# A decoder layer on one core: the scaling of the softmax weights of kv head 0, from DVE to ACT

## The chip, the core and the metric

The kernel runs on one core of one Trainium2 chip. Its engines work side by side, each through its own queue: PE (TensorE, matrix products), DVE (VectorE, element by element), ACT (ScalarE, functions and copies with a scale), POOL (GpSimd) and SP (SyncE, which here issues the DMA transfers). They meet at semaphores. The metric is the device time of one execution in microseconds (us).

## What is computed

One layer: sliding-window attention and a short gated convolution side by side, merged by gates, then a gated feed-forward part. The change lies in the attention, with 8 query heads over 2 kv heads (4 query heads, `g`, to each kv head), blocks of 128 queries against 256 keys (the block before and its own), a band mask, and one more logit per head (the sink) in the softmax. Cut to that part:

```python
SEQ = 2048; HEAD_DIM = 64; N_HEADS = 8; N_KV_HEADS = 2; GROUP = 4; WINDOW = BLOCK = 128

scores = jnp.einsum("bnqhgd,bnkhd->bnhgqk", q, kw).astype(jnp.float32) * ATTN_SCALE
scores = jnp.where(mask[None, :, None, None], scores, -jnp.inf)
probs = jax.nn.softmax(jnp.concatenate([scores, sink], axis=-1), axis=-1)[..., :-1]
out = jnp.einsum("bnhgqk,bnkhd->bnqhgd", probs.astype(v.dtype), vw)
```

## The kernel before

Everything is float32; products are made from a high and a low part of each operand, in three matmuls (`mm3`, L247 to L249; `split` makes the two parts, a cast on ACT at L264 and a subtraction on DVE at L265). The sequence is cut into four chunks of 512 tokens. The kernel runs in stages: projections of the input (to about 700 us of the trace), four mixers, one to a chunk (to about 1130 us), the feed-forward part (the rest, PE nearly full all the way).

A mixer (`mixer`) goes over the chunk's four blocks of 128 queries. For block `b` it writes down `scores` of block `b`, then `weights_to_keys` and `attend` of block `b - 1`, and between these a number of steps of other work by a hand-written plan: the output projection of the chunk before (`out_proj`, tiles `wo`) and the conv branch of this chunk (`conv_steps`, tiles `brc`). Chunk 0 has no chunk before it, so its plan has the eight conv steps alone. When all four blocks are done, `attn_steps` multiplies the result with the attention branch's weights (tiles `bra`), gates it and splits it into `merged`. The weights of all these steps come by DMA, are split on ACT and DVE (tiles `wh`), and are fetched up to three tiles ahead.

`scores` takes the products of queries and keys in PSUM (`sc`), scales and masks them into `s` on DVE (L565; one tile `s` of 128 queries x 4 heads x 257 for each kv head, with the sink in the last column). For each kv head then: the maximum of each row, negated, on DVE (L574); `exp(s + m)` on ACT, a head at a time, with the sum of each row as a by-product (L576); the reciprocal of the sums on DVE (L578); and the scaling of the weights by it. For kv head 0 this is one multiply over all four heads on DVE (L580), for kv head 1 four copies with a scale on ACT (L584). In the first block of chunk 0 there are no earlier keys, so 128 columns to a head are scaled instead of 256. `weights_to_keys` turns the weights over on PE (L594) and splits them (`pts`), ACT and DVE again. `attend` multiplies them with the values (`po`, L607), adds the two halves of the result with a copy on ACT (L609) and an addition on DVE (L610) into `o`, and splits `o` into `attn`.

The program's text gives the dependencies; the order in which each engine takes its instructions is laid out by a planner when the kernel is built, with its own estimate of each instruction's time. An engine takes its instructions in that order and waits where the next one isn't ready. The tiles `s` and `pts` share a pool of eight buffers (`b4`); PSUM has eight.

Of the kernel before, what the change touches and what calls it, by code (L numbers as in the profile page):

```python
# [23 lines left out]
ALU = mybir.AluOpType  # L24
AF = mybir.ActivationFunctionType
AX = mybir.AxisListType

P = 128
# [6 lines left out]
NH, HD, G = 8, 64, 4  # L35
# [61 lines left out]
def layer_kernel(ctx: ExitStack, tc: tile.TileContext, x, w, bcol, g1, g2, gf, cw, fcw, sinks, out):  # L97
    nc = tc.nc
# [10 lines left out]
    def psum(name):  # L109
        return p_ps.tile([P, 512], F32, name=name, tag="ps")  # L110
# [440 lines left out]
    def scores(c, q, b):  # L551

        k0 = P if c == 0 and b == 0 else 0
        keys = slice(b * P + k0, b * P + 256)
        qs = slice(b * P, (b + 1) * P)
        ss = [pool["b4"].tile([P, G, 257], F32, name=f"s{c}_{b}_{kv}", tag="b4") for kv in range(2)]
        for kv in range(2):
            nc.scalar.copy(out=ss[kv][:, :, 256], in_=sinkb[:, kv * G:(kv + 1) * G])
        for hp in range(2):
            for kv in range(2):  # L560
                ps = psum(f"sc{c}_{b}_{hp}_{kv}").rearrange("p (h n) -> p h n", h=2)
                for h in range(2):
                    nc.tensor.matmul(ps[:, h, k0:], q[:, kv, hp * 2 + h, qs], kT[:, kv, keys], start=True, stop=False)
                    nc.tensor.matmul(ps[:, h, k0:], q[:, kv, hp * 2 + h, qs], kT[:, 2 + kv, keys], start=False, stop=True)
                nc.vector.scalar_tensor_tensor(out=ss[kv][:, hp * 2:hp * 2 + 2, k0:256], in0=ps[:, :, k0:],  # L565
                                               scalar=SCALE, in1=mask[:, None, k0:].to_broadcast([P, 2, 256 - k0]),
                                               op0=ALU.mult, op1=ALU.add)
        for kv in range(2):
            s = ss[kv]
            nm = f"{c}_{b}_{kv}"  # L570
            m = p_s.tile([P, G], F32, name=f"m{nm}", tag="m")
            den = p_s.tile([P, G], F32, name=f"den{nm}", tag="den")
            rden = p_s.tile([P, G], F32, name=f"rden{nm}", tag="rden")
            nc.vector.tensor_reduce(out=m, in_=s[:, :, k0:], axis=AX.X, op=ALU.max, negate=True)  # L574
            for g in range(G):
                nc.scalar.activation(out=s[:, g, k0:], in_=s[:, g, k0:], func=AF.Exp, bias=m[:, g:g + 1],  # L576
                                     accum_out=den[:, g:g + 1])
            nc.vector.reciprocal(out=rden, in_=den)  # L578
            if kv == 0:
                nc.vector.tensor_tensor(out=s[:, :, k0:256], in0=s[:, :, k0:256],  # L580
                                        in1=rden[:, :, None].to_broadcast([P, G, 256 - k0]), op=ALU.mult)
            else:
                for g in range(G):
                    nc.scalar.activation(out=s[:, g, k0:256], in_=s[:, g, k0:256], func=AF.Copy, scale=rden[:, g:g + 1])  # L584
        return ss

    def weights_to_keys(c, b, ss):
# [55 lines left out]
    def mixer(c, q, vT, conv, merged, beside):  # L643
# [12 lines left out]
        steps(plan[0])  # L656
        turn_v(c, vT)
        ss = scores(c, q, 0)
        steps(plan[1])
        for b in range(1, NT):  # L660
            nxt = scores(c, q, b)
            pts = weights_to_keys(c, b - 1, ss)
            steps(plan[2 * b])
            attend(c, b - 1, pts, attn)
            steps(plan[2 * b + 1])
            ss = nxt
# [404 lines left out]
```

## Time and profile before

| | us |
|---|---|
| median of 3 runs | 2549.35 |
| lowest of the runs | 2546.07 |
| the profiled execution | 2549.61 |
| its span, first to last instruction | 2546.4 |

One run of the three took 4931.02 us; the median does not rest on it.

In the profile's rows, a time in front is the start of an instruction (or of a group of like ones, `x4`) from the start of the span, and the next number how long the group took. In groups by line, the numbers behind the bar are the busy time of the group and the mean of one instruction in ns, then the idle time of the engine just before its instructions and what ended it. `out<-in` names the tiles. PEld is PE's loading of weights, which runs beside its matmuls. Instructions of one engine overlap a little: the next may begin before the last one ends.

### The profile page before, as it was taken

What the parts mean: (1) busy time and instruction counts of PE and PEld (TensorE: products, weight loads), DVE (VectorE), ACT (ScalarE), POOL (GpSimd) and SP (SyncE); (2) the same over time, 40 slices, a digit from 0 to 9 for tenths busy, and PEclk for the clock granted to TensorE, in tenths of its full rate; (3) what the DMA queues carried; (4) which work ended last, traced back from release to release, by engine and by line L of the source; (5) the groups of instructions that cost most, each with busy time, mean ns of one, the idle gap of its engine ahead of it and who ended that gap; (6) DMA issues with size and microseconds to landing.
All of it is one profiled execution on the core that took longest, in us unless ns stands there. A gap on an engine that the chain in (4) does not pass through costs nothing.

```text
span 2546.4 us, 30318 instructions
## 1 busy us (share of the span) xinstructions
PE 2470.5 (97%) x11032; PEld 2029.7 (80%) x11032; DVE 1782.3 (70%) x2282; ACT 1118.2 (44%) x1843; POOL 22.6 (1%) x72
## 2 busy tenths in 40 slices
PE   7999999999989998998999999999999999999998
PEld 6888787888868787876788888888888888888886
DVE  6977746664388676677788888755478888875335
ACT  5545544444466353544555555422135555551001
POOL 0000000000000000000000000000000000000000
PEclk9999999999999999999999999999999999999999
DMA  4656897233568868688543233788463332356421
GB/s 154 192 184 206 272 345 226 92 108 100 176 223 306 285 236 288 229 272 306 207 151 131 100 117 115 294 319 295 175 231 124 109 123 100 108 191 258 179 83 66
DMA packets 191221, 488.66 MB, mean 192 GB/s; under 512 B 22112, under 2 KB 41696, under 8 KB 181728
## 3 DMA queue, kind: packets, MB, share of 16 engines
q1 hardware_dynamic: 191072, 486.73, 55.1%
q8 instruction: 86, 1.41, 0.2%
q14 instruction: 63, 0.52, 0.1%
HBM read 325.17 MB, written 161.48 MB: 191 GB/s over the span
## 4 chain that ended last, share of the span: by engine, by line
PE 81%; DMA 7%; DVE 5%; ACT 3%; issue 3%; SPq 2%; POOL 0%; POOLq 0%; DVEq 0%; ACTq 0%
PE upx L792 10%; PE upx L793 9%; PE upx L794 9%; PE dn L249 6%; PE dn L247 6%; PE dn L248 6%; PE upz L794 5%; PE upz L792 5%; PE upz L793 5%; PE upy L793 2%; PE upy L792 2%; PE upy L794 2%; DMA hb<-hd 2%; PE wo L247 2%; PE wo L249 2%
## 5 line engine op out<-in xcount | busy, mean ns | idle before, releaser
L792 PE MATMUL upx<-upx,wh 128*128 128x512 f32 x704 | 277.0, 394 | 5.8 <-ACT u L815 3.9
L793 PE MATMUL upx<-upx,wh 128*128 128x512 f32 x704 | 276.2, 392 | 0.0
L794 PE MATMUL upx<-upx,wh 128*128 128x512 f32 x704 | 275.9, 392 | 0.1
L247 PE MATMUL dn<-act,wh 128*128 128x512 f32 x704 | 274.3, 390 | 0.0
L249 PE MATMUL dn<-act,wh 128*128 128x512 f32 x704 | 274.0, 389 | 0.0
L248 PE MATMUL dn<-act,wh 128*128 128x512 f32 x704 | 273.9, 389 | 0.0
L895 DVE TENSOR_TENSOR hr<-dn,hr 128x512 f32<-128x512 f32 x192 | 131.3, 689 | 199.3 <-PE dn L249 199.1
L853 DVE SCALAR_TENSOR_TENSOR a<-u,fcwc,a 128x1024 f32<-128x1024 f32 x176 | 224.0, 1282 | 49.8 <-ACT a L851 47.0
L264 ACT CAST wh<-ws 128x1024 fp32r<-128x1024 f32 (+1 forms) x150 | 124.9, 834 | 142.3 <-DVE ws L207 67.1
L264 ACT CAST wh<-wr 128x1024 fp32r<-128x1024 f32 (+1 forms) x72 | 69.6, 975 | 261.4 <-PE dn L249 218.9
L792 PE MATMUL upx<-x,wh 128*128 128x512 f32 x440 | 173.2, 394 | 6.5 <-ACT u L824 3.6
L265 DVE TENSOR_TENSOR wh<-ws,wh 128x1024 fp32r<-128x1024 f32 (+1 forms) x150 | 143.1, 955 | 45.5 <-ACT wh L264 45.2
L793 PE MATMUL upx<-x,wh 128*128 128x512 f32 x440 | 172.2, 391 | 0.0
L794 PE MATMUL upx<-x,wh 128*128 128x512 f32 x440 | 172.1, 391 | 0.1
L792 PEld LDWEIGHTS upx<-upx,wh 128*128 128x128 f32 x704 | 132.6, 188 | 37.2 <-ACT u L815 4.3
L794 PEld LDWEIGHTS upx<-upx,wh 128*128 128x128 f32 x704 | 132.5, 188 | 29.8 <-DVE wh L265 0.5
L793 PEld LDWEIGHTS upx<-upx,wh 128*128 128x128 f32 x704 | 132.5, 188 | 28.4
L248 PEld LDWEIGHTS dn<-act,wh 128*128 128x128 f32 x704 | 132.2, 188 | 27.6
L249 PEld LDWEIGHTS dn<-act,wh 128*128 128x128 f32 x704 | 132.1, 188 | 27.6
L247 PEld LDWEIGHTS dn<-act,wh 128*128 128x128 f32 x704 | 132.1, 188 | 27.0
L793 PE MATMUL upz<-upx,wh 128*128 128x512 f32 x352 | 137.1, 389 | 0.8 <-DVE upx L265 0.8
L792 PE MATMUL upz<-upx,wh 128*128 128x512 f32 x352 | 137.1, 389 | 0.0
(274 smaller groups left out, 5394.4 us busy)
## 6 DMA issues: line engine op xcount, KB each, us to landing
act<-actd SPq DMA_DIRECT2D x20, 2048.0 KB, 9.5
wrb<-in_w_dram SPq DMA_DIRECT2D x75, 512.0 KB, 3.7
wra<-in_w_dram SPq DMA_DIRECT2D x75, 512.0 KB, 3.7
wr<-in_w_dram SPq DMA_DIRECT2D x64, 512.0 KB, 5.9
actd<-ach SPq DMA_DIRECT2D x88, 256.0 KB, 2.2
actd<-acl SPq DMA_DIRECT2D x88, 256.0 KB, 2.4
upx<-upd SPq DMA_DIRECT2D x10, 2048.0 KB, 9.7
sgd<-u SPq DMA_DIRECT2D x64, 256.0 KB, 2.9
```

The costliest lines, as they stand in the source:

```text
L247: nc.tensor.matmul(ps, ah, bh, start=start, stop=False)
L248: nc.tensor.matmul(ps, ah, bl, start=False, stop=False)
L249: nc.tensor.matmul(ps, al, bh, start=False, stop=stop)
L264: nc.scalar.copy(out=dh, in_=src)
L265: nc.vector.tensor_sub(out=dl, in0=src, in1=dh.bitcast(F32))
L792: nc.tensor.matmul(bank, ah, bh, start=start and k == 0, stop=False, skip_group_check=True)
L793: nc.tensor.matmul(bank, ah, bl, start=False, stop=False, skip_group_check=True)
L794: nc.tensor.matmul(bank, al, bh, start=False, stop=stop and k == 3, skip_group_check=True)
L853: nc.vector.scalar_tensor_tensor(out=a, in0=u[:, k:k + 2 * T], scalar=w3[k], in1=a, op0=ALU.mult, op1=ALU.add)
L895: nc.vector.tensor_tensor(out=hs[n][j], in0=ps, in1=hs[n][j], op=ALU.add)
```

## The change

The distinction between the two kv heads is gone: both are scaled by four copies on ACT, each with the head's reciprocal as its scale.

```diff
             nc.vector.reciprocal(out=rden, in_=den)
-            if kv == 0:
-                nc.vector.tensor_tensor(out=s[:, :, k0:256], in0=s[:, :, k0:256],
-                                        in1=rden[:, :, None].to_broadcast([P, G, 256 - k0]), op=ALU.mult)
-            else:
-                for g in range(G):
-                    nc.scalar.activation(out=s[:, g, k0:256], in_=s[:, g, k0:256], func=AF.Copy, scale=rden[:, g:g + 1])
+            for g in range(G):
+                nc.scalar.activation(out=s[:, g, k0:256], in_=s[:, g, k0:256], func=AF.Copy, scale=rden[:, g:g + 1])
         return ss
```

There are 16 blocks (four chunks of four), so 16 multiplies on DVE go and 64 copies on ACT come.

## The prediction

> **What bounds the kernel now.** I read the page first, then busy time by windows over the part in which the changed lines run, then the lists of ACT, DVE and PE in order of time. Of the page:
>
> ```profile
> span 2546.4 us, 30318 instructions
> PE 2470.5 (97%) x11032; PEld 2029.7 (80%) x11032; DVE 1782.3 (70%) x2282; ACT 1118.2 (44%) x1843; POOL 22.6 (1%) x72
> PE 81%; DMA 7%; DVE 5%; ACT 3%; issue 3%; SPq 2%; POOL 0%; POOLq 0%; DVEq 0%; ACTq 0%
> ```
>
> TensorE is busy 97% of the span and carries 81% of the chain that ended last. DVE is busier than ACT (70% against 44%), but DVE has only 5% of the chain and ACT 3%, so moving work between them is worth what happens in those few places. The changed lines run between 708 and 1110 us, in the four mixers. Windows over the attention part of each (chunk 0, 1, 2, 3), then over three stretches between chunks (columns: window, its length, busy us and instructions of PE, PE's weight loads, DVE, ACT and POOL, granted clock, busy share of the DMA engines, GB/s):
>
> ```profile
> 708.00:757.00 49.00, 37.83 (x192) 28.83 (x192) 44.08 (x71) 40.07 (x121) 0.00 (x0) 0.97 0.57 203
> 777.00:865.00 88.00, 87.86 (x450) 73.75 (x450) 72.28 (x108) 56.97 (x145) 1.38 (x1) 1.00 0.82 287
> 900.00:988.00 88.00, 88.00 (x457) 74.66 (x457) 63.66 (x99) 50.97 (x137) 1.39 (x1) 1.00 0.68 237
> 1020.00:1110.00 90.00, 89.33 (x463) 76.00 (x464) 66.02 (x103) 50.09 (x132) 1.38 (x1) 1.00 0.65 229
> ```
> ```profile
> 865.00:890.00 25.00, 19.75 (x77) 14.79 (x76) 14.25 (x22) 3.00 (x5) 0.00 (x0) 0.93 0.89 304
> 965.00:1015.00 50.00, 43.45 (x192) 34.69 (x193) 31.44 (x51) 15.07 (x37) 1.39 (x1) 0.97 0.91 319
> 1115.00:1165.00 50.00, 43.83 (x176) 34.78 (x175) 37.77 (x54) 20.23 (x30) 0.00 (x0) 0.93 0.88 300
> ```
>
> Two kinds of attention stage. In chunks 1 to 3 PE has no room to gain: 0.14, 0.00 and 0.67 us idle, because the plan puts the last chunk's output projection and the conv branch beside the softmax. In chunk 0 that filling is thin: PE stands 11.2 of 49 us, DVE is busy 44.1 and ACT 40.1. There the softmax itself sets the time. Between chunks PE waits with the DMA engines busy 88 to 91%; the change touches no transfer.
>
> **The instructions and their prices.** Groups by line, shapes kept apart:
>
> ```profile
> L584 ACT ACTIVATE s<-s,rden 128x256 f32<-128x256 f32 x60 | 25.6, 498 | 0.5 <-DVE rden L578 0.5
> L580 DVE TENSOR_TENSOR s<-s,rden 128x1024 f32<-128x1024 f32 x15 | 18.2, 1216 | 0.1
> ```
> ```profile
> L580 DVE TENSOR_TENSOR s<-s,rden x16: 679/1214/1225, 712.7 to 1088.4; 128x1024 f32<-128x1024 f32 x15, 128x512 f32<-128x512 f32 x1
> ```
> ```profile
> 713.52 1.28 ACT L584 ACTIVATE s<-s,rden 128x128 f32<-128x128 f32 x4 [0.39 <-DVE rden L578]
> ```
>
> Removed: 16 DVE multiplies (L580), 15 of 1.22 us and one, half as wide, of 0.68 (block 0 of chunk 0, which has no earlier keys). Added: 64 ACT copies with a scale, 60 of 128x256 and four of 128x128. One takes 498 ns by itself but they overlap: 25.6 us for 60 is 0.43 each, and four in the list below go from 722.25 to the next start at 723.86, 1.61 us. So a block costs ACT 1.61 (1.28 for the four narrow ones) and saves DVE 1.22. Over all: DVE 15 x 1.22 + 0.68 = 19.0 us less, ACT 15 x 1.61 + 1.28 = 25.4 us more. No transfer is added, and the function is one that ACT already runs between the exponentials.
>
> [...] Counting that loss against DVE (1.61 - 1.22) as time in each of 16 blocks would give 6.2 us more, 2555.8; that lies within the range that the rows give below.
>
> **Chunk 0, block by block.** ACT's list, blocks 1 and 2 (their exponentials start at 716.95 and 727.79):
>
> ```profile
> 716.47 0.58 ACT L264 CAST pts<-pt 128x512 fp32r<-128x512 f32 x1 [1.21 <-PE pt L594]
> 716.95 0.51 ACT L576 ACTIVATE s<-s,m 128x257 f32<-128x257 f32 x1
> ...
> 721.03 1.19 ACT L609 COPY o<-po 64x512 f32<-64x512 f32 x2
> 722.25 1.71 ACT L584 ACTIVATE s<-s,rden 128x256 f32<-128x256 f32 x4
> 723.86 0.60 ACT L264 CAST attn<-o 128x512 fp32r<-128x512 f32 x1
> ...
> 726.47 0.64 ACT L264 CAST wh<-wr2attn 128x512 fp32r<-128x512 f32 x1
> ...
> 727.79 0.51 ACT L576 ACTIVATE s<-s,m 128x257 f32<-128x257 f32 x1
> ...
> 732.35 1.71 ACT L584 ACTIVATE s<-s,rden 128x256 f32<-128x256 f32 x4
> 734.08 0.58 ACT L609 COPY o<-po 64x512 f32<-64x512 f32 x1
> ...
> 739.85 0.51 ACT L576 ACTIVATE s<-s,m 128x257 f32<-128x257 f32 x1 [2.60 <-DVE m L574]
> ```
>
> and DVE's over block 2:
>
> ```profile
> 730.57 1.22 DVE L580 TENSOR_TENSOR s<-s,rden 128x1024 f32<-128x1024 f32 x1
> 731.87 0.18 DVE L578 RECIPROCAL rden<-den 128x4 f32<-128x4 f32 x1
> ...
> 734.69 0.69 DVE L610 TENSOR_TENSOR o<-po,o 64x512 f32<-64x512 f32 x1 [0.28 <-ACT o L609]
> 735.41 1.29 DVE L565 SCALAR_TENSOR_TENSOR s<-sc,mask 128x512 f32<-128x512 f32 x2
> ...
> 738.61 2.34 DVE L574 TENSOR_REDUCE m<-s 128x4 f32<-128x1028 f32 x2
> ```
>
> The lists are not in the order of the text: both maxima (L574) stand together, and kv 1's exponentials follow kv 0's without waiting. A planner orders each engine. So I do not assume that ACT stops after kv 0's exponentials; the new copies go in after some of kv 1's, when the reciprocal is there. The new wait is ACT's for the reciprocal on DVE; behind it on ACT stand kv 1's exponentials, the o copies and the pts casts, and PE's transposes (L594) wait for those.
>
> Block 0: 1.28 us of copies; ACT then idles 1.21 us before 716.47, waiting for PE, and the 0.39 us wait for the reciprocal, which stands behind the multiply, goes. I take 0, ends 0 and 1.28.
> Block 1: ACT has no idle from 716.95 to 727.79, so 1.61 is the upper end. But the weight casts at 726.47 and behind can slip into the later 2.60 us idle, which leaves about 0.3. I take 0.8.
> Block 2: the loop from one block's exponentials to the next is read backwards: 739.85 waits for the maximum at 738.61, DVE is full back to 734.69, which waited for ACT's o copy at 734.08, which stood behind the copies at 732.35. DVE's multiply at 730.57 is beside this, not on it; the added copies are on it: 1.61. With the multiply gone the last po of the earlier block is ready some 1.2 earlier, and its copy could go ahead of the scale copies: then 0. I take 0.8.
> Block 3 has no later scores; its ACT list has no room:
>
> ```profile
> 743.92 0.58 ACT L609 COPY o<-po 64x512 f32<-64x512 f32 x1
> 744.41 1.71 ACT L584 ACTIVATE s<-s,rden 128x256 f32<-128x256 f32 x4
> ...
> 746.74 1.56 ACT L264 CAST pts<-pt 128x512 fp32r<-128x512 f32 x3
> ```
>
> From the copies the way leads over transposes and casts to the attn cast for which PE waits before the attention branch. I take 1.6, ends 0 and 1.61.
> Gain: if DVE were the only limit of the stage, four multiplies gone are worth 0.68 + 3 x 1.22 = 4.3 us. I take 0, since the backward reading finds none of them on the way; 4.3 is the lower end.
>
> **Chunks 1 to 3.** The first block of chunk 1 is tight:
>
> ```profile
> 791.37 1.71 ACT L584 ACTIVATE s<-s,rden 128x256 f32<-128x256 f32 x4
> ```
> ```profile
> 791.31 2.58 PE L594 MATMUL pt<-ident,s 128*128 128x128 f32 x16
> 793.65 0.48 PE L247 MATMUL wo<-mg,wh 128*128 128x512 f32 x1
> ```
>
> PE's transposes run while the copies are still being made; 1.61 us more on ACT can hold PE 1.61 us, or nothing if the planner puts wo matmuls first. I take 0.8. In the later blocks the cover is large, as chunk 2 shows (copies first, transposes of the same block second):
>
> ```profile
> 912.68 1.69 ACT L584 ACTIVATE s<-s,rden 128x256 f32<-128x256 f32 x4
> ...
> 923.57 1.71 ACT L584 ACTIVATE s<-s,rden 128x256 f32<-128x256 f32 x4 [0.25 <-DVE rden L578]
> ```
> ```profile
> 916.14 1.91 PE L594 MATMUL pt<-ident,s 128*128 128x128 f32 x16
> ```
> ```profile
> 938.22 1.75 PE pt L594 x16
> ```
>
> (The last row is from the chain.) Block 0 has 916.14 - (912.68 + 1.69) = 1.77 us, just more than 1.61, and kv 1's transposes are the later eight; block 1 has 938.2 - 925.3 = 12.9 us. These cost 0. Were that cover gone, each block would cost up to 1.61.
>
> **Sum.** The profiled execution took 2549.6 us, 3.2 around its span of 2546.4; the median of the runs is 2549.35, so it stands for them. 0 + 0.8 + 0.8 + 1.6 + 0.8 = 4.0: 2549.6 + 4.0 = 2553.6. Ends of the direct costs: 2549.6 - 4.3 = 2545.3, and 2549.6 + 1.28 + 4 x 1.61 = 2557.3.
>
> **Rivals.**
> 1. DVE's relief decides chunk 0. For it: DVE is busy 44.1 of 49 us there. Against it: the way back from 739.85 goes through ACT. 2545.3. Chance 0.13.
> 2. Nothing changes: the planner lays the copies into ACT's idle time (1.21 and 2.60 in chunk 0) and moves the o copies ahead. 2549.6. Chance 0.17.
> 3. The planner lays out the rest differently. For it: order is its own, and transfers start when buffers come free. The three stretches between chunks hold 5.3, 6.6 and 6.2 us of PE idle with DMA at 88 to 91%; a changed start of transfers can take away or add some of these 18 us. If half: 2549.6 + 4.0 plus or minus 9, 2544.6 or 2562.6. Chance 0.17, split evenly.
> 4. Slower by far: ACT stands in every block until the reciprocal has come through DVE's queue, behind one maximum (half of 2.34) and two mask additions (1.29), with PE waiting for it. 1.61 + 1.17 + 1.29 + 0.18 = 4.25 in each of 16 blocks, 68 us: 2618. It passes 2% from 3.2 us a block. Against it: the 12.9 us of cover. Chance 0.03.
>
> **How the numbers follow.** The forecast keeps 0.5. Two per cent of 2549 is 51 us, about what a measurement of this kernel can tell from no change; PE's whole idle time is 2546.4 - 2470.5 = 75.9 us, only 11 of it in chunk 0, so a gain of that size has 0.01 at most. Rival 4 gives slower 0.03; all else is within: 0.96. The range of 8 in 10 takes in the direct ends and most of rival 3: 2544 to 2562; the forecast's own is 2549.6 to 2557.3.
>
> **What would show it.** After the change: DVE 18 to 19 us less busy, ACT some 25 us more; 128 scale copies in place of 64; the window of chunk 0's attention 3 us longer with ACT busier than DVE in it; PE idle in chunks 2 and 3 as before. Wrong would be: chunk 0 shorter (rival 1), or chunk 0 unchanged and the difference lying between the chunks or behind 1165 us (rival 3), or transposes in chunks 2 and 3 waiting for scale copies (rival 4).

## The result, and the profile after

| | before | after |
|---|---|---|
| median, us | 2547.93 (5 runs) | 2561.39 (5 runs, 2558.26 to 2566.92) |
| profiled execution, us | 2549.61 | 2562.91 |
| its span, us | 2546.4 | 2560.3 |

The ratio is 1.0052, with a 95% interval of 1.0040 to 1.0063: by 2% the same, but measurably slower, by 13.4 us between the medians. One of the five runs before took 4931.02 us, and two runs of the experiments took over 3500 us (one of them a profile, not used below): the ratios and their intervals leave such runs out.

The page of the changed kernel, span, busy time of the engines and the chain:

```profile
span 2560.3 us, 30359 instructions
PE 2475.7 (97%) x11032; PEld 2033.5 (79%) x11032; DVE 1765.9 (69%) x2266; ACT 1141.6 (45%) x1907; POOL 21.5 (1%) x72
PE 83%; DMA 6%; DVE 4%; ACT 3%; issue 2%; SPq 2%; POOL 0%; POOLq 0%; DVEq 0%; ACTq 0%
```

The change did what it says: DVE has 16.4 us and 16 instructions less, ACT 23.4 us and 64 instructions more. PE's own work is the same, but its busy time is 5.2 us more, a first sign that some of its matmuls ran slower.

Where the time went is read from stages. The attention of a chunk is taken here from the first matmul that turns the values over (`vp`, L548) to the first one of the attention branch (`bra`). Windows over it for chunks 0 and 1, before and then after (start and end of the window, its length, busy us of PE, weight loads, DVE, ACT, POOL, granted clock, share of the DMA engines, GB/s):

```profile
702.83:754.24 51.41, 40.24 (x214) 31.26 (x212) 46.55 (x76) 42.09 (x124) 0.00 (x0) 0.97 0.59 211
776.15:868.33 92.18, 90.86 (x466) 76.08 (x464) 73.79 (x110) 58.02 (x145) 1.38 (x1) 1.00 0.82 292
```
```profile
705.88:759.77 53.89, 40.09 (x214) 31.21 (x212) 42.85 (x72) 48.00 (x140) 0.00 (x0) 0.97 0.57 202
781.70:879.24 97.54, 92.58 (x465) 77.20 (x464) 71.17 (x108) 63.79 (x162) 1.01 (x1) 0.98 0.78 274
```

and for chunks 2 and 3 after:

```profile
912.90:1003.80 90.90, 90.17 (x466) 76.19 (x464) 61.13 (x97) 57.22 (x153) 1.01 (x1) 1.00 0.69 240
1035.60:1125.30 89.70, 89.70 (x466) 76.32 (x464) 61.23 (x98) 55.93 (x147) 1.01 (x1) 1.00 0.64 217
```

Chunk 0 is 2.5 us longer, and ACT is now the busier engine in it (48.0 against 42.9). Chunk 1 is 5.4 us longer: PE idles 4.96 us instead of 1.32, and is busy 1.72 longer with the same matmuls. Chunks 2 and 3 have the lengths that they had (90.8 and 89.7), with 6 us more on ACT each.

Chunk 1 shows how it goes. ACT in order of time: the two groups of copies of block 0 (795.33 for kv head 0, 799.34 for kv head 1), then block 1, of whose exponentials only the first of kv head 1 is shown (those of kv head 0 start at 802.94):

```profile
795.33 1.69 ACT L580 ACTIVATE s<-s,rden 128x256 f32<-128x256 f32 x4
...
799.34 1.71 ACT L580 ACTIVATE s<-s,rden 128x256 f32<-128x256 f32 x4
...
804.92 1.04 ACT L264 CAST pts<-pt 128x512 fp32r<-128x512 f32 x2
805.86 1.71 ACT L580 ACTIVATE s<-s,rden 128x256 f32<-128x256 f32 x4
807.47 0.49 ACT L576 ACTIVATE s<-s,m 128x257 f32<-128x257 f32 x1
...
809.44 0.56 ACT L264 CAST pts<-pt 128x512 fp32r<-128x512 f32 x1
809.91 1.71 ACT L580 ACTIVATE s<-s,rden 128x256 f32<-128x256 f32 x4
```

and PE over the same stretch (what ended an idle time stands in brackets):

```profile
797.35 1.03 PE L590 MATMUL pt<-ident,s 128*128 128x128 f32 x8
799.90 0.44 PE L590 MATMUL pt<-ident,s 128*128 128x128 f32 x2 [1.51 <-ACT s L580]
...
806.34 1.10 PE L603 MATMUL po<-pts,vt 128*128 128x512 f32 x4
810.06 0.62 PE L603 MATMUL po<-pts,vt 128*128 128x512 f32 x1 [2.61 <-ACT pts L264]
810.47 0.63 PE L247 MATMUL wo<-mg,wh 128*128 128x512 f32 x1
810.90 0.63 PE L248 MATMUL wo<-mg,wh 128*128 128x512 f32 x1
```

Two waits. PE has turned over kv head 0 of block 0 and stands 1.51 us for kv head 1's copies, which are late by kv head 0's. Then the third cast of `pts` (block 0, kv head 1), whose transposes were done at about 801, is taken by ACT only at 809.44: the planner has put block 1's scale copies and the exponentials of its kv head 1 ahead of it, 805.86 to 809.44, 3.6 us. PE stands 2.61 us for it. In the kernel before, all four casts stood together ahead of block 1's first exponential:

```profile
794.96 2.00 ACT L264 CAST pts<-pt 128x512 fp32r<-128x512 f32 x4
...
797.76 0.51 ACT L576 ACTIVATE s<-s,m 128x257 f32<-128x257 f32 x1 [0.60 <-DVE m L574]
```

A third part comes behind the second wait. Three windows of 3.4 us, laid where the trace's records of the granted clock change, the first with the wait in it:

```profile
806.90:810.30 3.40, 0.79 (x4) 0.38 (x3) 0.94 (x3) 3.40 (x12) 0.00 (x0) 1.00 0.97 261
810.30:813.70 3.40, 3.40 (x9) 2.65 (x9) 1.76 (x3) 3.38 (x8) 0.00 (x0) 0.50 0.78 307
813.70:817.10 3.40, 3.40 (x16) 2.75 (x16) 2.73 (x5) 2.38 (x6) 0.00 (x0) 1.00 0.62 255
```

After a stretch with PE busy 0.79 of 3.40 us the granted clock is 0.50 for the next 3.4 us; the two `wo` matmuls above start 0.43 us apart, where in the profile before they start 0.23 apart. Nine matmuls pass instead of sixteen: about 1.7 us, as PE's busy time in the stage says too (1.72 more). So 1.51 + 2.61 + 1.7 = 5.8; PE's other idle time in the stage is 0.5 us less than before (0.84 against 1.32), and the stage is 5.4 longer.

### The profile page after: what moved, and what is told of

Its sections match the earlier page's. It is cut to its first block, busy times and chain, and to the rows that moved or that the text cites. A ratio compares the mean times of both kernels' runs of the same rounds, so it can differ in the third digit from the quotient of the medians.

```text
span 2560.3 us, 30359 instructions
## 1 busy us (share of the span) xinstructions
PE 2475.7 (97%) x11032; PEld 2033.5 (79%) x11032; DVE 1765.9 (69%) x2266; ACT 1141.6 (45%) x1907; POOL 21.5 (1%) x72
## 4 chain that ended last, share of the span: by engine, by line
PE 83%; DMA 6%; DVE 4%; ACT 3%; issue 2%; SPq 2%; POOL 0%; POOLq 0%; DVEq 0%; ACTq 0%
PE upx L788 10%; PE upx L789 10%; PE upx L790 10%; PE dn L247 6%; PE dn L248 6%; PE dn L249 6%; PE upz L790 5%; PE upz L788 5%; PE upz L789 5%; PE upy L790 2%; PE upy L789 2%; PE upy L788 2%; PE wo L247 2%; PE wo L249 2%; PE wo L248 2%
```

## The experiments

Theory A: ACT's added copies cost time where PE has nothing else to do until they are through, in chunk 0 and in the first two blocks of chunk 1, and nowhere else. Rival B: the planner's other layout of transfers behind the attention, which any edit brings. Rival C: DVE's relief is worth something. Lengths in us of the stages, as defined above, from each kernel's profile, and the ratios (95% interval) to runs of the kernel before taken beside it:

| kernel | start of chunk 0 | chunk 0 | 1 | 2 | 3 | ratio |
|---|---|---|---|---|---|---|
| before | 702.8 | 51.4 | 92.2 | 90.8 | 89.7 | |
| before_again | 706.4 | 49.9 | 92.3 | 90.7 | 89.6 | a profile alone |
| after | 705.9 | 53.9 | 97.5 | 90.9 | 89.7 | 1.0052 (1.0040 to 1.0063) |
| rep | 705.1 | 56.2 | 97.8 | 91.5 | 89.7 | 1.0049 (1.0030 to 1.0069) |
| c0_only | 706.5 | 56.5 | 92.5 | 91.0 | 89.7 | 1.0023 (1.0011 to 1.0035) |
| c1_only | 705.2 | 50.7 | 97.5 | 91.4 | 89.8 | 1.0019 (1.0006 to 1.0033) |
| c23_only | 708.1 | 51.2 | 92.5 | 91.2 | 89.8 | 1.0010 (0.9998 to 1.0022) |
| pts_first | 709.7 | 56.2 | 93.6 | 91.2 | 89.7 | 1.0023 (1.0013 to 1.0034) |
| c1b0_only | 700.9 | 51.1 | 94.7 | 91.0 | 89.7 | 1.0004 (0.9995 to 1.0014) |
| c1b1_only, profile of c1b1_again | 703.7 | 50.7 | 91.0 | 90.7 | 89.6 | 0.9996 (0.9987 to 1.0005) |
| dve_heads0 | 704.0 | 52.6 | 92.1 | 91.7 | 89.7 | 1.0014 (1.0001 to 1.0027) |
| c0_kv0_unscaled | 705.9 | 50.8 | 91.6 | 90.6 | 89.7 | 1.0003 (0.9994 to 1.0012) |
| c0_kv1_unscaled | 707.0 | 49.5 | 91.3 | 91.1 | 89.6 | 1.0001 (0.9992 to 1.0011) |

**rep**: the changed kernel with four blank lines, so that lines keep their numbers; L584 is then L580.

> The changed kernel once more, with four blank lines so that its line numbers are those of the kernel before. Against the kernel before the changed one took 13.4 us more by the medians. Between the two profiles 2 to 3 us of difference lie ahead of 703 us, where the instructions of all engines stand in the same order. If that part is run-to-run variation, this profile has it at another size (0 to 1 us) and the rest the same: 2.5 us more in the attention of chunk 0, 5.3 in that of chunk 1, about 1.0 in the attention branch of chunk 1, 1.6 between 1113 and 1250 us. If it belongs to the kernel, the 2 to 3 us come again. Time 2558 to 2564 either way.

The 5.4 us of chunk 1 came again (5.6). Chunk 0 was 4.8 longer than in the first profile of before, not 2.5. The start of chunk 0 was later again, by 2.3 us (3.1 the first time), against the 0 to 1 that was expected of variation; before_again, further down, tells what that is. The 1.0 us in the attention branch of chunk 1 did not come again: from its first matmul to the start of chunk 2 it took 32.6 us before, 33.6 after and 30.9 in rep.

**The change in one part of the chunks alone**, three kernels that differ in a condition:

```diff
-            if kv == 0:
+            if kv == 0 and c > 0:      # c0_only
+            if kv == 0 and c != 1:     # c1_only
+            if kv == 0 and c < 2:      # c23_only
```

> Kv head 0 goes to ACT in chunk 0 alone. Theory A (the cost lies where ACT stands in PE's way, in chunk 0 and the first two blocks of chunk 1): 2.5 us more than before, all of it in the attention of chunk 0, so about 2550.5. Rival B (the cost is a different layout of the transfers behind, and any edit brings it): 8 us or more, beyond chunk 0. Rival C (DVE's relief is worth something): less than before.

> Kv head 0 goes to ACT in chunk 1 alone. Theory A: 5.3 us more than before in the attention of chunk 1 (1.5 of PE waiting for a scale copy, 2.6 waiting for a cast of pts behind copies and exponentials on ACT, and slower matmuls right after that wait), and perhaps 1 us in its attention branch: about 2553 to 2554. Rival B: 8 us or more, most of it elsewhere. Rival C: 0 or less.

> Kv head 0 goes to ACT in chunks 2 and 3 alone. Theory A: 0 in the attention of both chunks, since PE has matmuls of the output projection and the conv branch until the copies are done; 2548, within 1.6 for what comes behind. Rival B: 3 us or more, between the chunks or behind 1130 us. A fourth, that every block costs something: 6 us or more in the windows of attention.

Each pays in its own chunk and nowhere else in attention: 56.5 in chunk 0 (twice the 2.5 that was expected), 97.5 in chunk 1, nothing in 2 and 3. The ratios 0.23, 0.19 and 0.10% add up to 13.3 us of 2552, the whole change to 12.5 by rep. So the cost lies in separate places, and rival B is not needed for chunks 0 and 1. The 0.10% of c23_only has zero in its interval; it isn't in the attention of any chunk, and where it lies stays open.

**pts_first**: the changed kernel, with block 0's transposes and casts written down ahead of block 1's softmax, in chunk 1 alone.

```diff
-    def scores(c, q, b):
+    def scores(c, q, b, between=None):
...
+        pts = weights_to_keys(c, b - 1, between) if between else None
         for kv in range(2):
             s = ss[kv]
...
-            nxt = scores(c, q, b)
-            pts = weights_to_keys(c, b - 1, ss)
+            if (c, b) == (1, 1):
+                nxt, pts = scores(c, q, b, ss)
+            else:
+                nxt = scores(c, q, b)
+                pts = weights_to_keys(c, b - 1, ss)
```

> The changed kernel, with one thing moved in chunk 1: the transposes and splits of block 0 (weights_to_keys) are written down before the softmax of block 1, so that ACT takes the four casts of pts before the exponentials and copies of block 1. All 64 copies stay on ACT. Theory A (of the 5.3 us in chunk 1, PE's wait for the third cast of pts, which stands behind four copies and four exponentials on ACT, makes some 4 with the slow matmuls after it): the attention of chunk 1 costs 1.5 us more than before instead of 5.3, and the time is about 4 us under that of the changed kernel. Rival (the copies' time on ACT as such holds PE, wherever they stand): still 4 to 5.3 us. A wait of 2.6 us on a cast of pts must be gone from PE's waits under A.

ACT's list of this kernel in chunk 1, with all four casts together and the exponentials and copies of block 1 behind them:

```profile
809.20 2.01 ACT L264 CAST pts<-pt 128x512 fp32r<-128x512 f32 x4
811.10 0.53 ACT L577 ACTIVATE s<-s,m 128x257 f32<-128x257 f32 x1
...
813.44 1.71 ACT L581 ACTIVATE s<-s,rden 128x256 f32<-128x256 f32 x4
```

and its PE, waits of 0.2 us and more between 782 and 835 us (who waited for what: us in all, times, longest):

```profile
PE pt L594 <- ACT s L581: 1.5, 1, 1.5
PE wo L248 <- DVE mg L265: 0.2, 1, 0.2
```

The 2.6 us wait is gone with the same 64 copies on ACT, and chunk 1 has 93.6 us, 1.5 over the profile of before and 4 under the changed kernel. The place of the copies in ACT's queue made that part, not their time. By the ratios the time is 6.6 us under rep's (0.26%), more than the 4 of the stage; the intervals of the two just overlap (1.0034 and 1.0030). What is left against the kernel before, 0.23% or 5.9 us, is about what chunk 0 and the first wait of chunk 1 cost.

**One block of chunk 1 alone:**

```diff
-            if kv == 0:
+            if kv == 0 and (c, b) != (1, 0):     # c1b0_only
+            if kv == 0 and (c, b) != (1, 1):     # c1b1_only, c1b1_again
```

> Kv head 0 on ACT in block 0 of chunk 1 alone, 4 copies instead of 64. Theory A: block 0's later copies make its transposes late, PE waits 1.5 us for them, and the casts of pts come after block 1's exponentials on ACT (without block 1's copies of kv head 0 in between, 1.6 us less than in the changed kernel). So the attention of chunk 1 is 2.5 to 4 us longer than before; the other stages as before. Rival (each block pays its own copies, 1.6): 1.6 us.

> Kv head 0 on ACT in block 1 of chunk 1 alone. Theory A: block 0's transposes come in time, ACT casts pts before block 1's exponentials, and block 1's copies have 13 us until their transposes: 0 us (within 0.5) in the attention of chunk 1. Rival (each block pays its own copies): 1.6 us.

> Kv head 0 on ACT in block 1 of chunk 1 alone, for an undisturbed profile. Theory A: 0 us (within 0.5) in the attention of chunk 1; rival: 1.6.

Four copies in block 0 cost 2.5 us of chunk 1's length, four in block 1 nothing: there the casts are all ahead of block 1's exponentials, as before, and the stage is even 1.2 us shorter, since PE's wait of 1.2 us for a weight tile at its end is missing in that profile. By their ratios, neither kernel's time differs from the kernel before. ACT's list in c1b0_only, with block 1's first exponential of kv head 1 between the casts, and its PE's waits from 770 to 830 us:

```profile
797.41 1.04 ACT L264 CAST pts<-pt 128x512 fp32r<-128x512 f32 x2
798.35 0.51 ACT L576 ACTIVATE s<-s,m 128x257 f32<-128x257 f32 x1
...
800.34 0.57 ACT L264 CAST pts<-pt 128x512 fp32r<-128x512 f32 x1
```
```profile
PE pt L594 <- ACT s L584: 1.5, 1, 1.5
PE po L607 <- DVE pts L265: 0.8, 1, 0.8
PE wo L248 <- DVE mg L265: 0.4, 1, 0.4
```

Here too the casts were put behind block 1's exponentials, but without block 1's extra copies the wait is 0.8 instead of 2.6. So block 0's lateness brings both the first wait and the bad order, and block 1's copies make the second wait long: alone the two blocks cost 2.5 and 0, together 5.4. The rival, that each block pays 1.6 us for its own copies, fails on block 1, which alone costs nothing.

**Chunk 0 from the other sides.** Both heads on DVE there, a head at a time (kv head 0 of the other chunks too):

```diff
-            if kv == 0:
-                nc.vector.tensor_tensor(...)
-            else:
-                for g in range(G):
+            for g in range(G):
+                if kv == 0 or c == 0:
+                    nc.vector.tensor_scalar(out=s[:, g, k0:256], in0=s[:, g, k0:256], scalar1=rden[:, g:g + 1], scalar2=None, op0=ALU.mult)
+                else:
                     nc.scalar.activation(out=s[:, g, k0:256], in_=s[:, g, k0:256], func=AF.Copy, scale=rden[:, g:g + 1])
```

> The other way round: in chunk 0 both kv heads, in chunks 1 to 3 kv head 0, are scaled on DVE a head at a time (a multiplication with one number for each row, 128x256), kv head 1 of chunks 1 to 3 stays on ACT. Theory A says that in chunk 0 ACT's copies lie on the way from one block's exponentials to the next and to the end: without them 2 to 4 us less in the attention of chunk 0 if the four narrow multiplies take no longer than the one wide (1.22 us), chunks 1 to 3 as before. Rival (DVE is the limit of chunk 0, busy 44 of 49 us there): 2 to 5 us more in chunk 0.

and, as two kernels, the scaling of one head left out in chunk 0 (`if kv == 0 and c == 0: pass` ahead; `elif c:` in place of `else:`), so that one engine loses work and the other gets none:

> The kernel before, with the scaling of kv head 0 left out in chunk 0 (its weights go on unnormalized there): DVE loses its four multiplies, ACT gets nothing. This is the relief of DVE by itself. If DVE sets chunk 0's time (rival 1 of the prediction), 2 to 4.3 us less in the attention of chunk 0. If ACT sets it (the prediction's backward reading), 0. With the 2.5 to 5 us that the copies on ACT cost there, the first would mean that the copies cost 5 to 9 us and give 2 to 4 back.

> The kernel before, with the scaling of kv head 1 left out in chunk 0: ACT loses its 16 copies there, DVE keeps its multiplies. If ACT's copies lie on the way through chunk 0 (the prediction's backward reading), 2 to 5 us less in its attention. If DVE holds it, 0 to 1. From the version with both heads on DVE, which was 1.2 us longer there with ACT 5 us less busy, I expect 0 to 2.

Freeing DVE of its four multiplies changed the time by nothing that can be told (ratio 1.0003), and freeing ACT of its 16 copies did not either (1.0001), though the stage itself, at 49.5, is at the low end there. With both heads on DVE, from which 2 to 4 us less were expected, chunk 0 took 52.6, no gain. So neither engine by itself holds the time of chunk 0, yet 6 us more on ACT cost 3 to 6 there. Rival C falls by the time, and so does half of the prediction's backward reading: the copies on ACT lie on the way once they are added, but nothing is gained by taking those that were there away. One thing stays open: in the profile without DVE's multiplies PE idled 7.7 us in chunk 0, against 9.7 to 11.2 in the six profiles with that chunk as before, but its matmuls took 43.1 us instead of 39.7 to 41.0, at a clock of 0.90. Less waiting was made up for by slower matmuls; whether that would be so in every run is not shown.

What the copies do to PE in chunk 0 is seen in its longest waits, of before (702 to 757 us) and then of rep (705 to 765 us):

```profile
PE po L607 <- DVE pts L265: 3.8, 4, 1.9
PE pt L594 <- DVE rden L578: 3.6, 1, 3.6
PE bra L247 <- ACT attn L264: 1.2, 1, 1.2
PE po L607 <- ACT pts L264: 1.2, 2, 0.7
```
```profile
PE pt L594 <- ACT s L580: 6.4, 4, 3.3
PE po L607 <- ACT pts L264: 3.2, 4, 1.4
PE po L607 <- DVE pts L265: 2.4, 2, 1.5
PE bra L247 <- ACT attn L264: 1.2, 1, 1.2
```

PE's waits move from DVE to ACT and grow, and the slow clock does the rest. The window of the same stage in rep:

```profile
705.12:761.29 56.17, 42.82 (x213) 33.11 (x211) 42.84 (x72) 48.12 (x140) 0.00 (x0) 0.91 0.56 198
```

Against before, PE idles 13.35 us instead of 11.17 (2.2 more) and is busy 42.82 instead of 40.24 (2.6 more, at a clock of 0.91 instead of 0.97). In the profile of after PE idled 2.6 us more, at a clock of 0.97, and the stage was 2.5 longer. That is the difference between the two profiles of one kernel: the idle time is alike (13.8 and 13.4), the slow stretches are not. Over all profiles of the table, the four with the change in chunk 0 idle 13.8 us there on average and the six with that chunk as before 10.2; their matmuls take 41.9 and 40.6. So of the 4.9 us by which the stage is longer, 3.5 are waits and 1.3 slower matmuls.

**before_again**: the kernel before, unchanged.

> The kernel before once more. In eight profiles the attention of chunk 0 began 1.9 us earlier to 6.9 us later than in the profile shown of before, with the same order of instructions ahead of it. If this is run-to-run variation, it shows here too, together with stretches of half clock of 3.4 us each after waits for transfers: 2 to 5 us later at the start of chunk 0, and 0.5 us or less of difference in the attention of chunks 0 to 3 taken by themselves.

Chunk 0 began 3.6 us later than in the first profile of the same kernel, and its attention was 1.5 shorter; the other chunks agreed within 0.1. So the 3 us ahead of chunk 0 in the first comparison were variation, and the expected 0.5 us was too narrow for chunk 0. A part of that variation is the clock again, here a stretch in the projections, first in the profile of before, then two in before_again, the first of which holds a wait of 2.8 us for ACT:

```profile
322.70:326.10 3.40, 3.40 (x17) 2.79 (x16) 0.69 (x1) 1.08 (x2) 0.00 (x0) 1.00 0.91 266
```
```profile
319.30:322.70 3.40, 1.09 (x5) 0.91 (x6) 3.07 (x5) 3.10 (x5) 0.00 (x0) 1.00 0.70 248
322.70:326.10 3.40, 3.40 (x10) 2.66 (x9) 1.23 (x1) 0.20 (x1) 0.00 (x0) 0.50 0.99 356
```

No version was measurably faster than the kernel before.

## Why the prediction was right, and where its sizes were not

The forecast was 2553.6 us in a range of 2544 to 2562, and no change by 2%; the time is 2561.39, at the upper edge. The likeliest case, with its own range to 2557.3, was too small by a factor of about three: 4.0 us against 13.4. That the time lies in the range all the same is luck: above 2557.3 the range was there for rival 3, which looked for its cost in transfers between the chunks, and most of the cost came inside the attention.

- **The instructions and their prices: right in substance.** DVE lost 16.4 us by the page (19.0 forecast, without the overlap of neighbours), ACT gained 23.4 (25.4); the copies come in groups of four in 1.69 to 1.71 us as before.
- **The planner would put the copies among kv head 1's exponentials without ACT stopping: right.** In chunk 1 they follow the first of those, at 795.33.
- **Chunk 0, 3.2 us: the mechanism right, the size near, one part missing.** The mean over four profiles with the change in chunk 0 (53.9, 56.2, 56.5, 56.2) is 4.9 us over the mean of the six with chunk 0 as before (51.4, 49.9, 50.7, 51.2, 51.1, 50.7). The waits made 3.5 of it, near the 3.2; slower matmuls made 1.3, and the sum had no term for them. That DVE's relief gives no time there was right (c0_kv0_unscaled), though PE waited less. That ACT alone held the stage was not shown, and c0_kv1_unscaled speaks against it.
- **The first block of chunk 1, 0.8 us between 0 and 1.61: the term that failed.** The wait it meant, PE's for the later copies, is there at 1.51 us, the upper end. What it left out is that a late block 0 changes the order behind it: the casts of `pts` went behind block 1's copies and exponentials, 2.6 us of waiting, and 1.7 of slow clock. The prediction looked for the cover of block 1's own copies (12.9 us, read from chunk 2; it holds, c1b1_only costs nothing) and not at which other work they stand in front of on ACT, though it had named the pts casts among what is queued there. The stage cost 5.4, not 0.8; pts_first gives 4 of it back.
- **Chunks 2 and 3, 0 us: right**, within 0.7 us in each of the four profiles with the change there.
- **Rival 3, another layout behind the attention:** not needed for chunks 0 and 1, which make 4.9 + 5.4 = 10.3 of the 12.5 to 13.4 us. The rest is open. From the start of chunk 3's attention branch to the end, after had 1435.0 us and rep 1436.9, before 1433.2 and 1431.8; two profiles of one kernel differ there by 1.4 to 1.9 us, and the interval of c23_only reaches from -0.5 to 5.6 us.

## What to carry to other kernels

Work that is moved to an idle engine costs nothing only if the results of that engine for which the bound engine waits still come in time (ACT was busy 44% of the span before; its added copies cost nothing in the attention of chunks 2 and 3, and 5.4 us in chunk 1); look not at the engine's busy share but at what the moved instructions stand in front of in its queue. Where a planner lays out the order, a delay of 1.5 us in one block can change the order of the next one, so check the tight places (a first block, a stage with thin filling) by the order itself. And count a wait of TensorE of a few microseconds with the slow matmuls that may follow: here 2.6 us of waiting cost 4.3.

## What was not expected of the hardware

Behind a wait of 2.61 us, in a stretch with PE busy 0.79 of 3.40 us, the granted clock was 0.50 over the next 3.4 us. What goes with such a slow step in these traces is how busy PE was in the one step of 3.41 us of the clock's records before. In the 13 profiles of the table, between 300 and 2500 us, all 94 full-clock steps with PE busy under 1.45 us were followed by a step at half clock, and none of the 8082 with PE busy over 1.85 us was; between the two it was 22 of 65. So the length of a wait alone does not decide: in c0_kv1_unscaled a wait of 3.7 us fell across two steps, left PE busy 1.69 and 1.45 us in them, and no slow step followed. Such stretches also appear behind waits for transfers (in the profile of before, 3.25 us of waiting for a weight tile to 880.04 us, then a clock of 0.50 from 881.2 to 884.6) and not in the same places each time, and profiles of one kernel differ by some microseconds (the start of chunk 0 lay between 700.9 and 709.7 us in the profiles above, with the same order of instructions ahead of it). A difference of a few microseconds between two single profiles is told apart only stage by stage, and with a second profile of the same kernel beside it.
